# The experts' stage of a hybrid encoder layer: down products moved behind the next pair's gate and up, and a second tile for one expert alone

## The chip, the cores and the metric

The kernel runs on one core of one Trainium2 chip. The metric is the time of one execution on the device in microseconds (us); 1420.89 us is the median of three runs before the change. Engines are called by their short names: PE (TensorE, matrix products), PEld (its weight loads), DVE (VectorE), ACT (ScalarE), POOL (GpSimd), SP (SyncE, which here issues transfers).

## The reference

The layer mixes tokens (neighbourhood attention beside a gated delta rule) and then sends each of 1024 tokens to two of 64 SwiGLU experts. Only the second half bears on the change:

```
def hierarchical_moe(h, wg_r, bg_r, we_r, be_r, w_gate, w_up, w_down):
    ...
    top_val, top_idx = lax.top_k(in_group, TOP_K_IN_GROUP)      # 2 of 8 experts of the token's group
    gates = gp * jax.nn.softmax(top_val, axis=-1)
    ...
    def expert_block(args):
        tok, e = args
        xb = h_pad[tok]                                          # rows of 1024
        hid = jax.nn.silu(xb @ w_gate[e]) * (xb @ w_up[e])       # 256 wide
        return hid @ w_down[e]
    ...
    y = jnp.zeros((n + 1, d_), h.dtype).at[buf_tok].add(out)[:n]
```

All weights are float32: gate and up of an expert are 2 MiB together, down is 1 MiB, so 64 experts are 192 MiB.

## The kernel before

Up to about 840 us the kernel does token mixing and routing. What follows is the experts' stage, a loop of 32 steps (`NS`). Step i takes a **pair** of experts, e and e + 32, which belong to different groups; the first tile of a pair is 128 rows, 64 (`CAP`) for each expert. For a step the kernel

- gathers the rows of the tokens by an indirect transfer that POOL issues (`gather`, L1020), three steps ahead (`LA = 3`) into four buffers `xgb`;
- transposes them on PE into `xT` (`turn`, L1028), with DVE copying out of PSUM (L1029);
- multiplies by gate and up (`pp`, L1042): 8 slices of the inner dimension for each expert, the two experts of a slice one after the other on the two column halves of PE;
- forms silu(gate) * up (`sg`, ACT L1047 and DVE L1048), transposes it (`ph`, L1051; `hT`, ACT L1053);
- multiplies by down (`po`, L1060), scales by the gate weight (`yg`, DVE L1062), and adds the rows into the output by an indirect transfer with accumulation (L1063, POOL).

`experts` writes all of this. Its argument `between` is the transposes of the next step's rows, which are written behind the gate and up products; in the last step it is None, and then the products are ordered by expert (L1040) instead of alternating:

```
        if between is None:
            order.sort(key=lambda kd: kd[1])
```

If one expert of the pair has more than 64 tokens (`more[i] > CAP`, L1112), a **second tile** follows at the end of the step: `experts` once more with 128 rows for both experts, out of the same buffer `xgb` (L1086, L1113). By the counts that the reference's own inputs give, this happens in steps 0, 8, 15, 19, 23 and 24; in step 15 both experts have more than 64 tokens, in the five others one has. Every engine evaluates the branch in every step.

**Loads.** SP issues the weights. Gate and up go into seven buffers (`wg`), down into six (`wd`), `room = (7, 6)`. Experts 0 to 4 are loaded before the loop; POOL issues three loads at its start, because in step 0 `eng` is pool. Then each step issues four, in an order set by `loads`: wg, wd, wd, wg. A load waits until the products that read its buffer are done, those of a second tile too, and until the load eight places ahead of it has landed.

Of the kernel before, what the change touches and what calls it, by code (L numbers as in the profile page):

```python
# [19 lines left out]
P = 128  # L20
# [16 lines left out]
def tile_layer(ctx, tc, a, out):  # L37
# [930 lines left out]
    for f, t in [(None, 0)] + tail:  # L968
        ins = f(t) if f else last
        if f is None or f is ao_mm and t in (4, 6, 7):  # L970
            e = pace.pop(0)
            wt.setdefault(e % 32, []).append(load_w(mwA, e, after=ins))
        if f is ao_mm and t == NT - 1:

            opj.close()
            mwB = ctx.enter_context(tc.tile_pool(name="mwB", bufs=1, side="right", reuse_waits="tile"))
            m1 = ctx.enter_context(tc.tile_pool(name="m1", bufs=1, side="right", reuse_waits="tile"))
            wt.setdefault(steps[2][1], [[], []])[0] += load_w(mwB, steps[2][1], after=ins)
            tS = [m1.tile([P, 32, 4], I32, name=f"tS{i}") for i in range(2)]
# [4 lines left out]
            for x in xgb:  # L984
                pool.memset(x, 0.0)

    for tl in range(2):
        for d in range(2):
            src = tab[tl * CAP:(tl + 1) * CAP, d * 32:(d + 1) * 32]
            dst = tS[tl][d * 64:(d + 1) * 64]  # L990
            dve.tensor_scalar(dst[:, :, 0], src[:, :, 0], OOB, None, op0=OP.add)
            dve.tensor_copy(dst[:, :, 2:4].bitcast(F32), src[:, :, 1:3])
# [4 lines left out]
    ci = cst.tile([1, 128], I32, name="ci")  # L997
# [4 lines left out]
    dve.tensor_tensor(ci[:, 0:32], cnt[:, 0:32], cnt[:, 32:64], op=OP.max)  # L1002
    pool.iota(lim, pattern=[[CAP, 14]], base=2 * CAP, channel_multiplier=0, allow_small_or_imprecise_dtypes=True)
# [29 lines left out]
    def experts(ws, meta, xT, gp, between=None):  # L1033
# [7 lines left out]
        for k, d in order:  # L1041
            pe.matmul(pp[d * CAP:(d + 1) * CAP], xT[:, k, d * CAP:(d + 1) * CAP],  # L1042
                      ws[d][0][:, :, k * 256:(k + 1) * 256], start=(k == 0), stop=(k == NK - 1))
# [4 lines left out]
        dve.scalar_tensor_tensor(sg[:n], pp[:n, 1], mf[:n, 3:4], sg[:n], op0=OP.mult, op1=OP.mult)  # L1048
        ph = psX.tile([P, 2, P], F32, name="ph", bufs=1)
# [3 lines left out]
        act.activation(hT[:, :, :n], ph[:, :, :n], AF.Copy)  # L1053
        yg = m2.tile([P, D], F32, name="yg", bufs=3)
# [8 lines left out]
        ins = pool.indirect_dma_start(out=out, out_offset=bass.IndirectOffsetOnAxis(ap=meta[:n, 0:1], axis=0), in_=yg[:n],  # L1063
                                      in_offset=None, bounds_check=S - 1, oob_is_err=False, compute_op=OP.add)
        if gp is None:
            return
        for g, ii in rows.items():
            if g != gp:
                for i in ii:
                    tc.declare_no_dep(ins.ins, i.ins, reason="rows of the tokens of other groups")  # L1070
        rows[gp].append(ins)
# [22 lines left out]
    second(0)  # L1094
    for i in range(NS):
        gp, e = steps[i]
        args = (pool, ins, mybir.DependencyClass.NoSync) if i == 0 else ()
        for n, part in loads[i and first + 4 * (i - 1):first + 4 * i]:
# [5 lines left out]

        def ahead():
            if i + 1 < NS:
                xTs[i + 1] = turn(xgb[(i + 1) % (LA + 1)], P)

        experts(wt[e], tS[0][:, e], xTs[i], gp, ahead if i + 1 < NS else None)
        if i + 1 < NS:  # L1110
            second(i + 1)
        with tc.If(more[i] > CAP):  # L1112
            experts(wt[e], tS[1][:, e], turn(xgb[i % (LA + 1)], P), gp, list)  # L1113
    rest = nc.values_load(ci[:, 32:33], min_val=0, max_val=S)
    with tc.If(rest > 0):
        with tc.For_i(0, 64) as e:
            left = nc.values_load(ci[:, bass.ds(e + 64, 1)], min_val=0, max_val=14)
            with tc.For_i(0, left) as i:
# [4 lines left out]
                experts([w], meta, turn(xgb[0], CAP), None)  # L1123
# [67 lines left out]
```

## Time and profile before

| | |
|---|---|
| three runs | 1419.18, 1420.89, 1422.25 us |
| the profiled execution | 1420.96 us; its span, first to last instruction, 1419.2 us |
| PE busy over the span | 1232.4 us (87%) |
| DVE, ACT, POOL busy | 658.2 us (46%), 393.8 us (28%), 378.1 us (27%) |
| loads of expert weights that SP issues | wg x62 (2048 KB each, median 34.5 us to landing), wd x63 (1024 KB, 33.5 us) |
| second tiles | 38 calls of L1047 and of L1063 for 32 steps: 6 |

Times in rows are counted from the span's start. "Landing" is the end of a transfer; a busy share is a mean over a stretch, and says nothing of what was waited for. The profiled execution stands 1.76 us above its span, and 0.07 us above the median of the runs.

### The profile page before, as it was taken

The numbers are of one execution on the slowest core, as the hardware profiler recorded it, in microseconds if no ns is written. First come the engines' busy times: TensorE is split into PE (matmuls) and PEld (weight loads), VectorE is DVE, ScalarE is ACT, GpSimd is POOL, SyncE is SP. The second block draws the span as 40 slices with busy tenths as digits, with TensorE's granted clock in tenths as the row PEclk, the third lists the DMA queues.
The fourth block names the chain that finished last, engine by engine and source line by source line (L and its number), as shares of the span: only waits on it lengthen the run. The fifth ranks groups of instructions, "written<-read, shape, count | busy, mean of one in ns | idle before, by whom it ended". The sixth has DMA issues, their size and how long they took to land. (4 is left out here: it accounts for less than half of the span.)

```text
span 1419.2 us, 20349 instructions
## 1 busy us (share of the span) xinstructions
PE 1232.4 (87%) x7313; PEld 829.9 (58%) x7314; DVE 658.2 (46%) x1629; ACT 393.8 (28%) x798; POOL 378.1 (27%) x428
## 2 busy tenths in 40 slices
PE   6987999969989996688989968998888989989985
PEld 6866889969978895466768843333322333323331
DVE  5566853753667652667867862222211221212211
ACT  6445422322344431766445310000000000000000
POOL 1147313021655544112210351211211121111200
PEclk9998999989999997799989979999999999999998
DMA  4251246346565469997793988999999999998981
GB/s 157 61 124 43 71 134 171 98 138 146 166 173 149 116 176 219 300 254 210 176 258 105 343 299 311 384 409 399 414 408 407 375 404 372 388 356 325 385 330 21
DMA packets 110134, 346.80 MB, mean 244 GB/s; under 512 B 43312, under 2 KB 49456, under 8 KB 93376
## 3 DMA queue, kind: packets, MB, share of 16 engines
q1 hardware_dynamic: 74480, 260.68, 51.0%
q0 software_dynamic: 27264, 68.80, 18.6%
q10 hardware_dynamic: 8272, 15.78, 3.1%
q8 instruction: 71, 1.16, 0.3%
q14 instruction: 47, 0.39, 0.1%
HBM read 305.26 MB, written 62.98 MB: 259 GB/s over the span
## 5 line engine op out<-in xcount | busy, mean ns | idle before, releaser
L1042 PE MATMUL pp<-wg,xT 128*64 128x512 f32 x1216 | 295.9, 615 | 35.8 <-DMA wg<-in_w_gu 21.0
L1042 PEld LDWEIGHTS pp<-wg,xT 128*64 128x64 f32 x1216 | 98.2, 141 | 227.9 <-issue 185.5
L1063 POOL DMA_INDIRECT out<-yg,tS x38 | 60.4, 1589 | 412.5 <-DVEq L1112 267.2
L1048 DVE SCALAR_TENSOR_TENSOR sg<-pp,tS,sg 128x256 f32<-128x256 f32 x38 | 18.4, 483 | 312.3 <-ACT sg L1047 312.3
L1060 PE MATMUL po<-wd,hT 128*64 128x512 f32 x608 | 140.5, 605 | 20.4 <-ACTq L1112 14.2
L1047 ACT ACTIVATE sg<-pp,tS 128x256 f32<-128x256 f32 x38 | 18.0, 474 | 483.4 <-PE pp L1042 483.4
L84 PE MATMUL pA<-w_hi,h_hi 128*128 128x256 f32 x512 | 150.4, 294 | 0.0
L85 PE MATMUL pA<-w_lo,h_hi 128*128 128x256 f32 x512 | 149.4, 292 | 0.0
L86 PE MATMUL pA<-w_hi,h_lo 128*128 128x256 f32 x512 | 149.4, 292 | 0.0
L1062 DVE TENSOR_SCALAR yg<-po,tS 128x512 f32<-128x512 f32 x76 | 57.0, 750 | 119.9 <-PE po L1060 119.9
L84 PEld LDWEIGHTS pA<-w_hi,h_hi 128*128 128x128 f32 x512 | 99.9, 195 | 0.7 <-issue 0.2
L86 PEld LDWEIGHTS pA<-w_hi,h_lo 128*128 128x128 f32 x512 | 99.7, 195 | 0.3
L85 PEld LDWEIGHTS pA<-w_lo,h_hi 128*128 128x128 f32 x512 | 99.8, 195 | 0.2
L1060 PEld LDWEIGHTS po<-wd,hT 128*64 128x64 f32 x608 | 40.6, 138 | 94.0 <-issue 66.4
L85 PE MATMUL pA<-h_lo,w_hi 128*128 128x512 f32 x192 | 77.4, 403 | 0.0
L84 PE MATMUL pA<-h_hi,w_hi 128*128 128x512 f32 x192 | 77.4, 403 | 0.0
L86 PE MATMUL pA<-h_hi,w_lo 128*128 128x512 f32 x192 | 76.8, 400 | 0.0
L76 DVE TENSOR_TENSOR w_lo<-w_raw,w_hi 128x512 fp32r<-128x512 f32 x56 | 38.7, 702 | 72.6 <-ACT w_hi L75 70.6
L250 DVE SCALAR_TENSOR_TENSOR acc<-raw,convw,acc 128x1024 f32<-128x1024 f32 x48 | 63.2, 1319 | 13.1 <-ACT acc L248 12.7
L84 PE MATMUL pA<-wo_hi,t_hi 128*128 128x512 f32 x128 | 55.1, 430 | 6.9 <-ACT t_hi L750 5.9
L1028 PEld LDWEIGHTS pt<-ident,xg 128*128 128x128 f32 x304 | 37.5, 195 | 37.6 <-issue 30.0
L665 PE MATMUL pv<-pT,vw 128*128 128x256 f32 x192 | 53.5, 415 | 2.5 <-ACT pT L656 1.6
(322 smaller groups left out, 2297.5 us busy)
## 6 DMA issues: line engine op xcount, KB each, us to landing
wg<-in_w_gu SPq DMA_DIRECT2D x62, 2048.0 KB, 34.5
wd<-in_w_down SPq DMA_DIRECT2D x63, 1024.0 KB, 33.5
bt<-in_bias SPq DMA_DIRECT2D x24, 384.0 KB, 5.5
w_raw<-in_w_nat SPq DMA_DIRECT2D x32, 256.0 KB, 3.4
w_raw<-in_w_dn SPq DMA_DIRECT2D x24, 256.0 KB, 3.4
k<-kk_d POOLq DMA_DIRECT2D x16, 384.0 KB, 10.2
SA_d<-cm POOLq DMA_DIRECT2D x8, 512.0 KB, 2.9
kk_d<-ev POOLq DMA_DIRECT2D x8, 512.0 KB, 4.4
```

Source lines behind the costliest of these rows:

```text
L76: dve.tensor_sub(lo[:, k:k + 2], raw, hi[:, k:k + 2].bitcast(F32))
L84: pe.matmul(dst, sh, mh, start=(i == 0), stop=False)
L85: pe.matmul(dst, sh, ml, start=False, stop=False)
L86: pe.matmul(dst, sl, mh, start=False, stop=(i == n - 1))
L250: dve.scalar_tensor_tensor(acc, raw[:, t:t + S], convw[:, m, t:t + 1], acc, op0=OP.mult, op1=OP.add)
L665: pe.matmul(pv, vw[:, w, half + g, pr * P:(pr + 1) * P], pT[:, g], start=(g == 0), stop=(g == 2))
L1028: pe.transpose(pt[:, k, :n], xg[:n, g * 4 + k:D:NK], ident[:n, :n])
L1042: pe.matmul(pp[d * CAP:(d + 1) * CAP], xT[:, k, d * CAP:(d + 1) * CAP], ws[d][0][:, :, k * 256:(k + 1) * 256], start=(k == 0), stop=(k == ...
L1048: dve.scalar_tensor_tensor(sg[:n], pp[:n, 1], mf[:n, 3:4], sg[:n], op0=OP.mult, op1=OP.mult)
L1060: pe.matmul(po[d * CAP:(d + 1) * CAP], hT[:, k, d * CAP:(d + 1) * CAP], w[1][:, k * D + c * 512:k * D + (c + 1) * 512], start=(k == 0), st ...
L1062: dve.tensor_scalar(yg[:n, cs], po[:n], mf[:n, 2:3], None, op0=OP.mult)
L1063: ins = pool.indirect_dma_start(out=out, out_offset=bass.IndirectOffsetOnAxis(ap=meta[:n, 0:1], axis=0), in_=yg[:n], in_offset=None, bound ...
```

## The change

A step is cut into `gate_up`, `turn_h`, `down` and `add_rows`. The down products of step i are now written behind gate and up of step i + 1 (`finish`). The second tile stands right behind gate and up of its own step, gathers into a buffer of its own (`xg2`, named xs) in two halves, and calls `second_tile` only for the expert that overflows: gate goes to one column half of PE and up to the other, 256 columns each, and the two halves of down's columns likewise. The list of loads is replaced by `upto`: the loads of a step are two wg and the two wd that came free one step later. `LA` is 2, `xT` has two buffers.

```
-            LA = 3
+            LA = 2
...
+            xg2 = m1.tile([P, D], F32, name="xs")
...
+    dve.tensor_copy(ci[:, 128:192], cnt)
...
-        xT = m2.tile([P, NK, P], F32, name="xT", bufs=3)
+        xT = m2.tile([P, NK, P], F32, name="xT")
...
-        order = [(k, d) for k in range(NK) for d in range(len(ws))]
-        if between is None:
-            order.sort(key=lambda kd: kd[1])
...
-        if between:
-            between()
+        for k in range(NK):
+            for d in range(len(ws)):
+                pe.matmul(pp[d * CAP:(d + 1) * CAP], xT[:, k, d * CAP:(d + 1) * CAP],
+                          ws[d][0][:, :, k * 256:(k + 1) * 256], start=(k == 0), stop=(k == NK - 1))
...
+    def second_tile(w, d, meta, xT, gp):
...
+        pp = psX.tile([P, 2, 256], F32, name="pp")
+        for k in range(NK):
+            for i in range(2):
+                pe.matmul(pp[hs[i], i], xT[:, k, mine], w[0][:, i, k * 256:(k + 1) * 256], start=(k == 0), stop=(k == NK - 1))
...
+        yg = m2.tile([P, D], F32, name="yg", bufs=3)
+        po = psX.tile([P, 512], F32, name="po")
+        for k in range(2):
+            for c in range(2):
+                pe.matmul(po[hs[c]], hT[:, k], w[1][:, k * D + c * 512:k * D + (c + 1) * 512],
+                          start=(k == 0), stop=(k == 1))
...
+        add_rows(yg[me], meta[me, 0:1], gp, (d,))
...
-    loads = [(2 * j + d, part) for j in range(2, NS) for part in range(2) for d in range(2)]
-    loads = [l for l in loads if l[0] != 4]
-    first = next(i for i, (n, part) in enumerate(loads) if n == room[part])
+    loaded = [[0, 1, 2, 3, 4], [0, 1, 2, 3, 4]]
+
+    def upto(i):
+
+        todo = []
+        for part in (1, 0):
+            n1 = min(2 * NS, room[part] + 2 * max(0, i - part))
+            todo += [(n, part) for n in range(2 * NS) if n < n1 and n not in loaded[part]]
+            loaded[part] += [n for n, p in todo if p == part]
+        return sorted(todo, key=lambda l: (l[0] + 3 * l[1], l[1]))
...
-            gather(xgb[i % (LA + 1)], tS[1][:, e], P)
+            for d in range(2):
+                gather(xg2[d * CAP:(d + 1) * CAP], tS[1][:, e + 32 * d], CAP)
...
+    def finish(i):
+        gp, e = steps[i]
+        down(wt[e], tS[0][:, e], hTs.pop(i), gp)
...
+        sg = gate_up(wt[e], tS[0][:, e], xTs.pop(i))
+        with tc.If(more[i] > CAP):
+            xT = turn(xg2, P)
+            for d in range(2):
+                c = nc.values_load(ci[:, 128 + e + 32 * d:129 + e + 32 * d], min_val=0, max_val=S)
+                with tc.If(c > CAP):
+                    second_tile(wt[e][d], d, tS[1][:, e + 32 * d], xT, gp)
         if i + 1 < NS:
             second(i + 1)
-        with tc.If(more[i] > CAP):
-            experts(wt[e], tS[1][:, e], turn(xgb[i % (LA + 1)], P), gp, list)
+        if i > 0:
+            finish(i - 1)
+        hTs[i] = turn_h(sg, P)
+        if i + 1 < NS:
+            xTs[i + 1] = turn(xgb[(i + 1) % (LA + 1)], P)
+    finish(NS - 1)
```

PE, one step in the steady part, before (L1042 gate and up, L1028 the next rows' transposes, L1084 and L1085 the branch on POOL's gather, L1051 and L1060 the step's own down, L1112 the branch of the second tile):

```order
L1042 MATMUL pp<-wg,xT 64x512 x16
L1028 MATMUL pt<-ident,xg_8039 128x128 x8
L1084 TENSOR_LOAD ci
L1085 COMPARE_AND_BRANCH
L1085 UNCONDITIONAL_BRANCH x2
L1051 MATMUL ph<-ident,sg 128x128 x2
L1060 MATMUL po<-wd,hT 64x512 x8
L1112 COMPARE_AND_BRANCH
L1028 MATMUL pt<-ident,xg_8038 128x128 x8
L1042 MATMUL pp<-wg,xT 64x512 x16
```

and now (L1076 the down products of the step before, L1051 the transposes for this step's own, L1029 the next rows, L1041 gate and up of the next step, L1155 its second tile, L1159 the expert):

```order
L1076 MATMUL po<-wd,hT 64x512 x8
L1051 MATMUL ph<-ident,sg 128x128 x2
L1029 MATMUL pt<-ident,xg_8038 128x128 x8
L1041 MATMUL pp<-wg,xT 64x512 x16
L1155 COMPARE_AND_BRANCH
L1029 MATMUL pt<-ident,xs 128x128 x8
L1158 TENSOR_LOAD ci
L1159 COMPARE_AND_BRANCH
L1089 MATMUL pp<-wg,xT 64x256 x16
L1095 MATMUL ph<-ident,sg_13485 128x64 x2
L1102 MATMUL po<-wd,hT_13491 64x512 x4
```

The second tile's branch, behind which the buffers of `wg` come free in a step without one, stood at the end of a step's down products and stands now right behind its gate and up.

SP, the last loads, before:

```order
L958 DMA wg<-in_w_gu 128x4096
L958 DMA wd<-in_w_down 128x2048 x2
L1085 COMPARE_AND_BRANCH
L1085 UNCONDITIONAL_BRANCH x2
L958 DMA wg<-in_w_gu 128x4096
L1112 COMPARE_AND_BRANCH
L1112 UNCONDITIONAL_BRANCH x2
L958 DMA wg<-in_w_gu 128x4096
L958 DMA wd<-in_w_down 128x2048 x2
```

and now:

```order
L958 DMA wd<-in_w_down 128x2048
L958 DMA wg<-in_w_gu 128x4096
L958 DMA wd<-in_w_down 128x2048
L958 DMA wg<-in_w_gu 128x4096
...
L1128 COMPARE_AND_BRANCH
L1128 UNCONDITIONAL_BRANCH x2
L958 DMA wd<-in_w_down 128x2048 x2
L1127 ISA x2
L958 DMA wd<-in_w_down 128x2048 x2
```

The last wg was third from the end with two wd behind it; now four wd stand behind it, and the four before alternate.

## Rows read from the trace of the kernel before

**Rows 1.** Busy time by stretches: PE, PEld, DVE, ACT, POOL, then clock, DMA, GB/s.
```profile
1050.00:1100.00 50.00, 39.82 (x166) 13.88 (x164) 9.54 (x15) 2.58 (x6) 8.78 (x7) 0.93 1.01 410
1375.00:1394.00 19.00, 18.16 (x64) 6.10 (x61) 3.18 (x5) 0.86 (x2) 1.56 (x1) 0.90 0.23 83
```

**Rows 2.** Waits of SP, 850 to 1420 us: total us, times, longest.
```profile
SPq L958 <- DMA wg<-in_w_gu: 203.6, 43, 6.7
SPq L958 <- PEq L1112: 88.7, 13, 11.4
```

**Rows 3.** Loads that SP issues, in order of time: start, us, count.
```profile
870.90 0.34 SPq L958 DMA_DIRECT2D wg<-in_w_gu  x1
...
890.91 12.01 SPq L958 DMA_DIRECT2D wg<-in_w_gu  x2
...
1021.84 5.98 SPq L958 DMA_DIRECT2D wg<-in_w_gu  x2
...
1240.08 6.24 SPq L958 DMA_DIRECT2D wg<-in_w_gu  x2
```

**Rows 4.** Time to landing by tile wg or wd: all wg, then single loads by window.
```profile
DMA to landing us min/median/max: 7.7/34.4/39.0
...
L958 POOL DMA_DIRECT2D wg<-in_w_gu x1: 558/558/558, 850.5 to 850.5; - x1
DMA to landing us min/median/max: 14.4/14.4/14.4
L958 SPq DMA_DIRECT2D wg<-in_w_gu x1: 328/328/328, 902.6 to 902.6; - x1
DMA to landing us min/median/max: 14.6/14.6/14.6
L958 SPq DMA_DIRECT2D wg<-in_w_gu x1: 328/328/328, 1354.8 to 1354.8; - x1
DMA to landing us min/median/max: 34.0/34.0/34.0
L958 SPq DMA_DIRECT2D wd<-in_w_down x1: 328/328/328, 1360.9 to 1360.9; - x1
DMA to landing us min/median/max: 32.9/32.9/32.9
```

**Rows 5.** PE in order of time: a second tile (step 8), then plain steps.
```profile
984.32 1.16 PE L1028 MATMUL pt<-ident,xg 128*128 128x128 f32 x8
985.84 7.09 PE L1042 MATMUL pp<-wg,xT 128*64 128x512 f32 x32 [0.36 <-DVE xT L1029]
994.05 0.51 PE L1051 MATMUL ph<-ident,sg 128*128 128x128 f32 x2 [1.12 <-DVE sg L1048]
995.09 3.65 PE L1060 MATMUL po<-wd,hT 128*64 128x512 f32 x16 [0.53 <-ACT hT L1053]
998.57 7.04 PE L1042 MATMUL pp<-wg,xT 128*64 128x512 f32 x32
...
1314.93 7.09 PE L1042 MATMUL pp<-wg,xT 128*64 128x512 f32 x32 [0.31 <-PEq L1112]
```

**Rows 6.** PE in order of time: step 0 and its second tile.
```profile
855.16 1.16 PE L1028 MATMUL pt<-ident,xg 128*128 128x128 f32 x8
863.79 7.09 PE L1042 MATMUL pp<-wg,xT 128*64 128x512 f32 x32 [0.42 <-DVE xT L1029]
```

**Rows 7.** PE in order of time: the end of the kernel.
```profile
1354.50 7.31 PE L1042 MATMUL pp<-wg,xT 128*64 128x512 f32 x32 [0.31 <-PEq L1112]
1372.87 9.97 PE L1042 MATMUL pp<-wg,xT 128*64 128x512 f32 x30 [3.78 <-SPq L1115]
1388.92 12.26 PE L1042 MATMUL pp<-wg,xT 128*64 128x512 f32 x32 [0.31 <-PEq L1112]
1403.30 3.65 PE L1060 MATMUL po<-wd,hT 128*64 128x512 f32 x16 [0.53 <-ACTq L1112]
```

**Rows 8.** The adding transfers, 900 to 1380 us, by tile: time to landing.
```profile
DMA to landing us min/median/max: 10.6/12.1/13.9
```

More of the change, by code (lines that the diff above doesn't have):

```diff
@@ L978, in tile_layer @@
             wt.setdefault(steps[2][1], [[], []])[0] += load_w(mwB, steps[2][1], after=ins)
-            tS = [m1.tile([P, 32, 4], I32, name=f"tS{i}") for i in range(2)]
+            tS = [m1.tile([P, 32, 4], I32, name="tS"), m1.tile([CAP, 64, 4], I32, name="t2")]
             ln2p = m1.tile([P, NK], F32, name="ln2p")
             act.dma_start(ln2p, a["ln2"][:, 1])
-            LA = 3
+            LA = 2
             xgb = [m1.tile([P, D], F32, name=f"xg{i}") for i in range(LA + 1)]
-            for x in xgb:
+            xg2 = m1.tile([P, D], F32, name="xs")
+            for x in (*xgb, xg2):
                 pool.memset(x, 0.0)
[L987 to L992, printed above, removed]
+    for tl, d in ((0, 0), (0, 1), (1, 0)):
+        src = tab[tl * CAP:(tl + 1) * CAP, d * 32:(d + 1 + tl) * 32]
+        dst = tS[tl][d * CAP:(d + 1) * CAP]
+        dve.tensor_scalar(dst[:, :, 0], src[:, :, 0], OOB, None, op0=OP.add)
+        dve.tensor_copy(dst[:, :, 2:4].bitcast(F32), src[:, :, 1:3])
     cnt = rc.tile([1, 64], F32, name="cnt")
@@ L996, in tile_layer @@
     over = o2.tile([P, D], F32, name="x2", bufs=5)[0:1, :64 * 14].rearrange("p (e i) -> p e i", i=14)
-    ci = cst.tile([1, 128], I32, name="ci")
+    ci = cst.tile([1, 192], I32, name="ci")
     pn = psQ.tile([P, P], F32, name="pv", bufs=1)
@@ L1031, in turn, with gate_up @@
         return xT
-    def experts(ws, meta, xT, gp, between=None):
+    def gate_up(ws, meta, xT):
         n = CAP * len(ws)
@@ L1053, in experts, with add_rows, down @@
         act.activation(hT[:, :, :n], ph[:, :, :n], AF.Copy)
+        return hT
+    def add_rows(yg, idx, gp, ds):
+        ins = pool.indirect_dma_start(out=out, out_offset=bass.IndirectOffsetOnAxis(ap=idx, axis=0), in_=yg,
+                                      in_offset=None, bounds_check=S - 1, oob_is_err=False, compute_op=OP.add)
+        if gp is None:
+            return
+        for g, ii in rows.items():
+            for i, di in ii:
+                if g != gp or not set(ds) & set(di):
+                    tc.declare_no_dep(ins.ins, i.ins, reason="rows of the tokens of other groups")
+        rows[gp].append((ins, ds))
+    def down(ws, meta, hT, gp):
+        n = CAP * len(ws)
+        mf = meta.bitcast(F32)
         yg = m2.tile([P, D], F32, name="yg", bufs=3)
@@ L1062, in experts @@
             dve.tensor_scalar(yg[:n, cs], po[:n], mf[:n, 2:3], None, op0=OP.mult)
[L1063 to L1070, printed above, removed]
@@ L1071, in experts @@
-        rows[gp].append(ins)
+        add_rows(yg[:n], meta[:n, 0:1], gp, (0, 1))
+    def second_tile(w, d, meta, xT, gp):
+        hs = [slice(0, CAP), slice(CAP, 2 * CAP)]
+        me, mine = hs[0], hs[d]
+        mf = meta.bitcast(F32)
+        pp = psX.tile([P, 2, 256], F32, name="pp")
+        for k in range(NK):
+            for i in range(2):
+                pe.matmul(pp[hs[i], i], xT[:, k, mine], w[0][:, i, k * 256:(k + 1) * 256], start=(k == 0), stop=(k == NK - 1))
+        sg = m2.tile([CAP, 256], F32, name="sg2", bufs=1)
+        act.activation(sg[:], pp[me, 0], AF.Silu, scale=mf[me, 3:4])
+        dve.scalar_tensor_tensor(sg[:], pp[hs[1], 1], mf[me, 3:4], sg[:], op0=OP.mult, op1=OP.mult)
+        ph = psX.tile([P, 2, P], F32, name="ph", bufs=1)
+        for k in range(2):
+            pe.transpose(ph[:, k, :CAP], sg[:, k:256:2], ident[me, me])
+        hT = m2.tile([P, 2, CAP], F32, name="hT2", bufs=1)
+        act.activation(hT, ph[:, :, :CAP], AF.Copy)
+        yg = m2.tile([P, D], F32, name="yg", bufs=3)
+        po = psX.tile([P, 512], F32, name="po")
+        for k in range(2):
+            for c in range(2):
+                pe.matmul(po[hs[c]], hT[:, k], w[1][:, k * D + c * 512:k * D + (c + 1) * 512],
+                          start=(k == 0), stop=(k == 1))
+        for c in range(2):
+            dve.tensor_scalar(yg[me, c * 512:(c + 1) * 512], po[hs[c]], mf[me, 2:3], None, op0=OP.mult)
+        add_rows(yg[me], meta[me, 0:1], gp, (d,))
@@ L1097, in tile_layer @@
         args = (pool, ins, mybir.DependencyClass.NoSync) if i == 0 else ()
-        for n, part in loads[i and first + 4 * (i - 1):first + 4 * i]:
+        for n, part in upto(i):
             f = steps[n // 2][1]
@@ L1122, in tile_layer @@
                 gather(xgb[0], meta, CAP)
-                experts([w], meta, turn(xgb[0], CAP), None)
+                down([w], meta, turn_h(gate_up([w], meta, turn(xgb[0], CAP)), CAP), None)
 def layout(inputs):
```

10 lines of the change are left out of this document (3 added, 7 removed).

## The prediction

> **What bounds the kernel now.** I read the stretches first [rows 1]. Around 1050 to 1100 us the DMA share is 1.01 at 410 GB/s while PE is busy for 39.82 of 50 us: the transfers are the scarce thing there. SP's waits say the same [rows 2]: 203.6 us of them are for an earlier load to land and 88.7 us for PE to pass the second tile's branch (L1112), so most loads are issued the moment another lands. Then the pace of the two sides. From the pair of wg loads at 1021.84 to the one at 1240.08 [rows 3] there are twelve steps, 18.19 us each, although two second tiles (steps 15 and 19) fell between. PE by itself needs (1354.50 - 1314.93) / 3 = 13.19 us for a step [rows 5, 7]. A second tile adds 998.57 - 984.32 = 14.25 us [rows 5], 85 us over all six, and the gaps it makes are absorbed as long as loads are queued: the median wg lands 34.4 us after its issue [rows 4], almost two steps.
>
> So the kernel's end is made of two pieces: when the last load lands, and what PE does after that. The last wd is issued at 1360.9 and lands 32.9 us later, at **1393.8** [rows 4]; the span ends at 1419.2, **25.4 us** later. In between, the DMA share is already low (0.23 in 1375 to 1394 [rows 1]), but landing is what PE waits for, and a load lands when its slowest part does: at 1372.87 PE goes on when a wg has landed that has two more wg and four wd behind it [rows 7].
>
> The rate of the load stream: the wg issued at 890.91 + 12.01 less its own third of a microsecond, that is 902.6, lands at 902.6 + 14.6 = 917.2 [rows 3, 4]; it belongs to expert 11 of the order, counted from 0. Behind it come wg 12 to 63 and wd 10 to 63, 52 * 2 + 54 = 158 MiB, in 1393.8 - 917.2 = 476.6 us: **3.02 us per MiB**, 18.1 per step, the same as SP's pitch. From 917 us on the stream never paused, so work taken off PE there moves nothing.
>
> **The change, part by part.**
>
> *Down moved behind the next gate and up.* Per step PE still has 32 + 16 matmul records, two and eight transposes. What goes are the 0.53 us before the down products (hT) and what comes is the wait for xT behind the transposes, 0.36 us [rows 5]; the branch's 0.31 us stays and its two inner branches stand inside a block that is skipped. About 13.1 us per step: nothing, hidden by the 18.1 us of loads. If that cover were gone the gain would be 0.1 us per step.
>
> *The second tile for one expert.* 256 columns per matmul do not occur in the trace. Below, half of 7.09 us is 3.55; above, the same 32 records at the same price, 7.09. The eight transposes with 128 columns take 1.16 us, 0.145 each [rows 5], which for 32 records is 4.6 us; I take that. With the rest of the tile (1.16 + 0.36 transposes, 1.12 + 0.51 + 0.53 around sg and hT, half of 3.65 for down, two branches at 0.31) it is 10.7 us against 14.25, and 19.3 for step 15, where it runs twice. PE saves 5 * 3.5 - 5 = 12 us, all but step 0 under the loads.
>
> *The start.* Here the loads do wait for PE. The last load that POOL issues, at 850.5, lands at 864.9 [rows 4]. The next one needs the buffer that step 0's second tile still reads, and that tile's gate and up run from 863.79 for 7.09 us [rows 6]; so it is issued at 870.90 [rows 3] and, by the shortest landing of all wg, 7.7 us [rows 4], is there at 878.6. From 864.9 to 917.2, 52.3 us, wg 7 to 11 and wd 6 to 9 come in, 14 MiB, which at 3.02 is 42.3: **10.0 us are lost**. Now the second tile starts where the transposes of the next rows stood, at 855.2 [rows 6], its rows being in a buffer of their own: 855.2 + 1.5 + 4.6 = 861.3 (860.2 to 863.8 by the bounds) frees the first buffer, 865.8 the second. wg 7 then lands about 869, wg 8 and the wd that POOL issues late, behind this branch, by 878; step 1's gate and up end about 875 and free the next. I find some 1.5 us still lost, so **8.5 us come back** (10 at most; 4 if the tile is at its dear bound and the branches' register loads cost a microsecond each). Later wd loads cost nothing: wd is needed a step later too, and is asked for two steps ahead as before. The last landing moves from 1393.8 to 1385.3.
>
> *The end.* Before, the last step's products were ordered by expert and took 12.26 us instead of 7.09, without overlap of the column halves; and gate and up of the step before, at the low clock after its wait, 9.97 us [rows 7]. The wg for the last step landed at 1354.8 + 34.0 = 1388.8, 5.0 us before the end of the stream [rows 4], so a MiB takes 2.5 us there. Now four wd stand behind the last wg: it lands 10 us before the last wd, the one before it 17.5 to 18. Counted from the last landing: gate and up of step 31 from -9.7 to -2.6, branch to -2.3, down of step 30 to +1.4, transposes +1.9, hT +2.4, down of step 31 to **+6.0**. Before, down ended at 1403.30 + 3.65 = 1406.95 and the span 12.25 us later (eviction, POOL, the adding transfer and the drain); that stays. The tail is 18.3 us; if the last gate and up take 9.97 because PE waited before them, 21.2. I take **19.6** against 25.4.
>
> *Costs elsewhere.* POOL has six indirect transfers in its step instead of four, two of them skipped with the second tile and two with its gather; its step is 18 us and a transfer there 1.6, so this is hidden. LA = 2 leaves the gather about two PE steps less a few microseconds, over 20 us. The yg buffers are a new wait: three are taken per step out of three, so the eviction of a step needs the adding transfer of the step before to have landed, 10.6 to 13.9 us after its issue [rows 8]. With two evictions (1.5) and POOL's start (0.3) that is a loop of 13.9, at most 15.7: above PE's 13.1, below 18.1. Nothing while loads bound; what is late is PE by 0.7 us a step in the first few steps, where loads are queued.
>
> **Sum** against the profiled execution (1420.96, 1.76 above its span; the median of the runs is 0.07 lower): span 1385.3 + 19.6 = 1404.9, time **1406.7 us**, 14.3 less: 8.5 from the start, 5.8 from the end. Its own range is 1403.9 - 1.0 to 1412.8 (10 and 18.3; 4 and 21.2 with a microsecond of scatter).
>
> **Rivals.** (A) *The start gives nothing*: POOL's late wd, or the nested branch, holds the early loads as long as now. For it: SP's 88.7 us on the branch show how a branch holds loads. Against: it is passed 10 us sooner. Time 1393.8 + 19.6 + 1.76 = 1415.2.
>
> [...]
>
> (C) *Slower*: the loop through yg becomes the bound. Its price from the point where it decides: an adding transfer that lands later than 16.3 us after its issue makes the loop longer than 18.1 us. For it: the transfers now share the queue with a stream that never pauses early, and POOL issues more. Against: the longest of 33 is 13.9 [rows 8], in the same saturated stretch. At 17.2 us, a loop of 19 us, 30 steps cost 0.9 each: 27 us against 14 gained, 1434.
>
> (D) *No change*: the loads take the time that they take, and a later first release eats the shorter tail: 1420.
>
> **How the numbers follow.** The sum's own case 0.55, A 0.14, B 0.08, C 0.10, D 0.08, and 0.05 for a gain larger than the sum's range (a stream without pauses that runs at 18.0 us a step, 1400). Faster by over 0.2% (under 1418.1; about what three runs can tell from no change, since they spread by 0.2%) is the sum, A, B and the larger gain, 0.82; within it 0.08; slower 0.10. The range goes to both neighbours, 1401 to 1418: it holds the sum's case, A, B and a part of D.
>
> **What would show it.** Right: the first SP load of the loop about 861 instead of 870.90, the pitch of wg pairs still 18.2, the last wd landing about 1385, four wd behind the last wg, gate and up of the last step near 7 us and down ending 6 us behind the last landing. Wrong: a pitch above 18.5, DVE's evictions waiting for out<-yg, PE waiting for xg or xs, or a gap in the landings between 865 and 900.

## The result, and the profile after

The changed kernel takes **1407.16 us** (median of four runs, 1401.6 to 1409.91) against 1421.16 for the kernel before on the same chip: a ratio of **0.9898, 95% interval [0.9864, 0.9932]**. Run again on another chip, it gave 1406.51 against 1419.18, 0.9909 [0.9894, 0.9925]; the experiments are compared with this second ratio, each by its own ratio to the kernel before on its own chip. The profiled execution took 1408.78 us, its span 1407.0. The forecast was 1406.7 us.

Five groups of rows of the profile after answer to those of before. First the costliest groups on the page (line, engine, operation, tiles, shape, count; busy us and mean ns of one; idle us just before them and what ended most of it):

```profile
L1041 PE MATMUL pp<-wg,xT 128*64 128x512 f32 x1024 | 233.1, 604 | 19.7 <-DVE xT L1030 19.4
L1076 PE MATMUL po<-wd,hT 128*64 128x512 f32 x512 | 126.8, 622 | 45.1 <-DVEq L1155 28.3
L1078 DVE TENSOR_SCALAR yg<-po,tS 128x512 f32<-128x512 f32 x64 | 47.0, 749 | 126.2 <-DMA out<-yg,tS 66.8
```

Of the 19.7 us that PE sits idle ahead of gate and up (L1041), 19.4 are for xT and none to speak of for wg; the down products (L1076) wait 28.3 us for DVE to pass the second tile's branch (L1155), and DVE's evictions (L1078) wait for the adding transfers. Next the loads that SP issues (start, us, count), which answer to [rows 3, 4]:

```profile
861.72 14.72 SPq L958 DMA_DIRECT2D wg<-in_w_gu  x3
...
1348.06 14.62 SPq L958 DMA_DIRECT2D wd<-in_w_down  x4
```

The first is issued at 861.72 instead of 870.90, and four wd stand behind the last wg. Then PE in step 0 (start, us; in brackets the idle time before it and its releaser):

```profile
848.41 7.89 PE L1041 MATMUL pp<-wg,xT 128*64 128x512 f32 x32
858.00 3.67 PE L1089 MATMUL pp<-wg,xT 128*64 128x256 f32 x32 [0.60 <-DVE xT L1030]
863.58 1.94 PE L1102 MATMUL po<-wd,hT 128*64 128x512 f32 x8 [0.37 <-ACT hT L1097]
```

The second tile for one expert has its gate and up done in 3.67 us, half of the 7.09 before [rows 6]. The busy time by stretches (PE, PEld, DVE, ACT, POOL, clock, DMA share, GB/s) answers to [rows 1]; the first fence is of before, three stretches that were not shown, the second of after:

```profile
860.00:900.00 40.00, 36.61 (x176) 14.16 (x174) 9.59 (x15) 2.58 (x6) 6.97 (x5) 1.00 0.82 298
1100.00:1150.00 50.00, 46.07 (x212) 17.62 (x210) 11.21 (x18) 3.44 (x8) 7.06 (x6) 0.97 0.99 378
1250.00:1300.00 50.00, 44.90 (x214) 17.08 (x212) 11.21 (x18) 3.43 (x8) 6.84 (x5) 1.00 0.86 321
```

```profile
860.00:900.00 40.00, 32.54 (x158) 14.80 (x156) 9.63 (x15) 2.85 (x7) 9.19 (x8) 0.97 1.00 386
1100.00:1150.00 50.00, 38.02 (x184) 15.50 (x182) 10.33 (x16) 3.21 (x8) 8.20 (x6) 0.90 0.93 355
1250.00:1300.00 50.00, 36.83 (x176) 14.74 (x178) 11.31 (x17) 2.46 (x6) 10.13 (x8) 0.87 0.89 338
1375.00:1386.00 11.00, 9.23 (x46) 3.42 (x42) 2.80 (x5) 0.86 (x2) 1.56 (x1) 1.00 0.19 59
1387.00:1391.00 4.00, 3.54 (x18) 1.25 (x14) 1.50 (x2) 0.36 (x1) 0.00 (x0) 1.00 0.00 0
```

Between 860 and 900 us the DMA share rose from 0.82 to 1.00: 0.18 * 40 = 7.2 us of transfers come earlier. Between 1250 and 1300 the stream is not full in either kernel, and between 1100 and 1150 it is not in the changed one. Nothing moves between 1387 and 1391: the last load has landed by 1387. Last PE at a plain step late in the loop and at the end, against [rows 5, 7]:

```profile
1336.12 7.09 PE L1041 MATMUL pp<-wg,xT 128*64 128x512 f32 x32 [0.33 <-DVE xT L1030]
1349.74 7.09 PE L1041 MATMUL pp<-wg,xT 128*64 128x512 f32 x32 [0.34 <-DVE xT L1030]
1378.16 7.09 PE L1041 MATMUL pp<-wg,xT 128*64 128x512 f32 x32 [1.02 <-DVE xT L1030]
1386.45 3.65 PE L1076 MATMUL po<-wd,hT 128*64 128x512 f32 x16 [1.20 <-DVEq L1155]
1391.08 3.65 PE L1076 MATMUL po<-wd,hT 128*64 128x512 f32 x16 [0.54 <-ACT hT L1053]
```

Here lies the surprise. No product at the end waits for a wg: the last step's gate and up wait for xT, and a plain step takes 13.6 us (1336.12 to 1349.74). So PE runs from step 25 to the end without a long wait for a load, though not always at that pace: the six steps from 1291.28 to 1378.16 take 14.5 us each on average. In the longest PE waits 2.32 us for xT, because DVE's evictions, which stand ahead of xT, waited 5.40 us for an adding transfer:

```profile
1304.81 1.41 DVE L1078 TENSOR_SCALAR yg<-po,tS 128x512 f32<-128x512 f32 x2 [5.40 <-DMA out<-yg,tS]
1306.87 8.78 PE L1041 MATMUL pp<-wg,xT 128*64 128x512 f32 x32 [2.32 <-DVE xT L1030]
```

The place where PE last waits for a load for long is step 23, which has a second tile. The rows of PE from there to step 25, and below them those of step 15, the other step with such a wait:

```profile
1233.26 8.12 PE L1041 MATMUL pp<-wg,xT 128*64 128x512 f32 x32 [0.34 <-DVE xT L1030]
1254.94 3.68 PE L1102 MATMUL po<-wd,hT 128*64 128x512 f32 x8 [6.66 <-DMA wd<-in_w_down]
1260.27 5.03 PE L1076 MATMUL po<-wd,hT 128*64 128x512 f32 x16 [1.65 <-DVEq L1159]
1291.28 7.09 PE L1041 MATMUL pp<-wg,xT 128*64 128x512 f32 x32 [0.34 <-DVE xT L1030]
```

```profile
1087.96 7.09 PE L1041 MATMUL pp<-wg,xT 128*64 128x512 f32 x32 [0.34 <-DVE xT L1030]
1107.15 3.68 PE L1102 MATMUL po<-wd,hT 128*64 128x512 f32 x8 [5.19 <-DMA wd<-in_w_down]
1124.57 7.09 PE L1041 MATMUL pp<-wg,xT 128*64 128x512 f32 x32 [0.34 <-DVE xT L1030]
```

The second tile needs its wd in its own step, while the first tile's down, moved, needs it one step later; the load had been put back for the latter, and PE waits 6.66 us. That the order of the loads causes this wait is read from the code and this row; no run puts that load forward again. The 8 records behind the wait take 3.68 us instead of the 1.94 of step 0, and the 16 behind those 5.03 instead of 3.65. The granted clock, the third figure from the end, is 1.00 over the 8 records of step 0, 0.50 over those behind the wait, and 0.72 over the 16: 0.50 up to 1263.00, 0.98 from there on.

```profile
863.58:865.52 1.94, 1.94 (x8) 0.48 (x8) 0.00 (x0) 0.00 (x0) 0.00 (x0) 1.00 0.86 355
1254.94:1258.62 3.68, 3.68 (x8) 0.82 (x8) 0.00 (x0) 0.00 (x0) 0.00 (x0) 0.50 1.02 430
1260.27:1265.30 5.03, 5.03 (x17) 1.62 (x17) 0.75 (x1) 0.00 (x0) 2.43 (x2) 0.72 0.69 262
```

With gate and up of steps 0, 15, 16, 23 and 25 in the kernel before, the difference of the two spans can be put together:

```profile
846.70 8.53 PE L1042 MATMUL pp<-wg,xT 128*64 128x512 f32 x32
1096.22 1.04 PE L1042 MATMUL pp<-wg,xT 128*64 128x512 f32 x2 [0.31 <-PEq L1112]
1126.83 7.04 PE L1042 MATMUL pp<-wg,xT 128*64 128x512 f32 x32
1240.63 1.04 PE L1042 MATMUL pp<-wg,xT 128*64 128x512 f32 x2 [0.36 <-PEq L1112]
1301.51 7.04 PE L1042 MATMUL pp<-wg,xT 128*64 128x512 f32 x32
```

Counted from step 0's gate and up (846.70 before, 848.41 after; the part ahead of it took 1.7 us longer in this execution), the gate and up of step 25 start at 1301.51 - 846.70 = 454.8 before and at 1291.28 - 848.41 = 442.9 after: 11.9 us earlier. From there to the span's end it is 117.7 us before and 115.7 after, 2.0 less. 11.9 + 2.0 - 1.7 = 12.2, the difference of the spans. Seven steps before the end most of the gain is made. It did not grow evenly: counted in the same way, the changed kernel is 10.0 us ahead at step 15, 4.0 at step 16 (behind the wait of 5.19 us for wd), 9.1 at step 23 and 11.9 at step 25.

### The profile page after: what moved, and what is told of

The parts are those of the page before. It is cut to its first block, busy times and chain, and to the rows that moved or that the text cites. A ratio compares the mean times of both kernels' runs of the same rounds, so it can differ in the third digit from the quotient of the medians.

```text
span 1407.0 us, 20840 instructions
## 1 busy us (share of the span) xinstructions
PE 1194.1 (85%) x7307; PEld 828.0 (59%) x7308; DVE 660.1 (47%) x1631; ACT 393.9 (28%) x800; POOL 387.4 (28%) x435
## 5 line engine op out<-in xcount | busy, mean ns | idle before, releaser
L1041 PE MATMUL pp<-wg,xT 128*64 128x512 f32 x1024 | 233.1, 604 | 19.7 <-DVE xT L1030 19.4
L1041 PEld LDWEIGHTS pp<-wg,xT 128*64 128x64 f32 x1024 | 74.4, 139 | 156.4 <-issue 128.2
L1076 PE MATMUL po<-wd,hT 128*64 128x512 f32 x512 | 126.8, 622 | 45.1 <-DVEq L1155 28.3
L1057 POOL DMA_INDIRECT out<-yg,tS x32 | 50.8, 1587 | 291.3 <-DVE yg L1078 242.8
L1045 DVE SCALAR_TENSOR_TENSOR sg<-pp,tS,sg 128x256 f32<-128x256 f32 x32 | 15.5, 484 | 233.2 <-ACTq L1155 189.0
L1076 PEld LDWEIGHTS po<-wd,hT 128*64 128x64 f32 x512 | 42.1, 142 | 129.5 <-issue 68.4
L1078 DVE TENSOR_SCALAR yg<-po,tS 128x512 f32<-128x512 f32 x64 | 47.0, 749 | 126.2 <-DMA out<-yg,tS 66.8
L250 DVE SCALAR_TENSOR_TENSOR acc<-raw,convw,acc 128x1024 f32<-128x1024 f32 x48 | 63.2, 1320 | 12.4 <-ACT acc L248 11.9
L1053 ACT ACTIVATE hT<-ph 128x256 f32<-128x256 f32 x32 | 12.3, 384 | 191.6 <-PE ph L1051 191.6
```

What stands on the lines that cost most here:

```text
L250: dve.scalar_tensor_tensor(acc, raw[:, t:t + S], convw[:, m, t:t + 1], acc, op0=OP.mult, op1=OP.add)
L1076: pe.matmul(po[d * CAP:(d + 1) * CAP], hT[:, k, d * CAP:(d + 1) * CAP], w[1][:, k * D + c * 512:k * D + (c + 1) * 512], start=(k == 0), st ...
L1078: dve.tensor_scalar(yg[:n, cs], po[:n], mf[:n, 2:3], None, op0=OP.mult)
```

## The experiments

The theories at the start: mine was the prediction's (an earlier first release in step 0 and a shorter tail; what second tiles cost later and where the down products stand is hidden under the loads); **R1**, the gain is PE time saved in all second tiles; **R2**, the gain is the move of the down products. After the second run came **T2**: PE, not the loads, sets the time from step 24 to the end.

All twelve runs, with the ratio to the kernel before and, in the last column, the distance in us to the changed kernel's 0.9909 (times 1420; the intervals of the two ratios together make that known to 3 to 4 us):

| run | median us | ratio, 95% interval | against the changed kernel |
|---|---|---|---|
| before, last step alternating | 1416.46 | 0.9983 [0.9968, 0.9998] | (-2.4 against before) |
| both experts' second tile, steps 8 to 24 | 1417.15 | 0.9989 [0.9973, 1.0005] | +11.4 |
| both experts' second tile, step 0 | 1412.13 | 0.9954 [0.9938, 0.9971] | +6.4 |
| down in its own step | 1411.41 | 0.9941 [0.9920, 0.9963] | +4.5 |
| changed kernel again | 1406.51 | 0.9909 [0.9894, 0.9925] | 0 |
| both tiles, steps 23 and 24 | 1413.14 | 0.9964 [0.9947, 0.9982] | +7.8 |
| both tiles, steps 8 and 19 | 1406.87 | 0.9919 [0.9899, 0.9938] | +1.4 |
| second tile's PSUM apart | 1408.03 | 0.9929 [0.9907, 0.9952] | +2.8 |
| its PSUM and its rows apart | 1409.98 | 0.9927 [0.9905, 0.9948] | +2.6 |
| last step by expert | 1410.96 | 0.9939 [0.9924, 0.9954] | +4.3 |
| down ahead of the branch | 1407.10 | 0.9916 [0.9900, 0.9932] | +1.0 |
| second tile whole, as before | 1419.92 | 1.0004 [0.9990, 1.0019] | +13.5 |

**The order of the last step.** In the kernel before:

```diff
-        experts(wt[e], tS[0][:, e], xTs[i], gp, ahead if i + 1 < NS else None)
+        experts(wt[e], tS[0][:, e], xTs[i], gp, ahead)
```

> The kernel before, with one difference: the last step's gate and up alternate between the two experts as in every other step, instead of being ordered by expert. My theory (a part of the gain is the shorter tail behind the last landing): gate and up of the last step take 7.1 us instead of 12.26, the last landing stays near 1394 us, so 5.2 us less, about 1416 us (1414 to 1417.5). Rival R1 (the gain is PE time saved in the six second tiles) and rival R2 (it is the place of the down products): neither is touched, so 1421 us, no change. A third way: the kernel's end hangs on the last wd alone and PE's order doesn't matter, also 1421.

Measured: -2.4 us by the ratio, -3.2 by the medians, half of the 5.2 forecast. And the same undone in the changed kernel:

```diff
-        for k in range(NK):
-            for d in range(len(ws)):
+        order = [(k, d) for k in range(NK) for d in range(len(ws))]
+        if apart:
+            order.sort(key=lambda kd: kd[1])
+        for k, d in order:
...
-        sg = gate_up(wt[e], tS[0][:, e], xTs.pop(i))
+        sg = gate_up(wt[e], tS[0][:, e], xTs.pop(i), i == NS - 1)
```

> The changed kernel, with the last step's gate and up ordered by expert again, as before the change. The prediction's tail term (12.26 instead of 7.09 us behind the last wg): +5 us, 1412. If the last wd's landing hides it (wd 63 lands when gate and up end plus 1.6 us): +3 to +4. No effect: 1407.

Measured: +4.3. PE at the end of the first run, then of the second:

```profile
1388.75 8.16 PE L1042 MATMUL pp<-wg,xT 128*64 128x512 f32 x32 [0.31 <-PEq L1112]
```

```profile
1376.40 12.29 PE L1043 MATMUL pp<-wg,xT 128*64 128x512 f32 x32 [0.34 <-DVE xT L1030]
```

In the kernel before the alternating burst takes 8.16 us, so 12.26 - 8.16 = 4.1 could be had; in the changed one it is 12.29 against 7.09. That term stands, at 2 to 4 us as measured, with an uncertainty of 2 to 3.

**Second tiles where they might be hidden, and the start.** The inner branch of the changed kernel, in steps after 0, in step 0 alone, in steps 23 and 24, and in 8 and 19:

```diff
-                with tc.If(c > CAP):
+                with tc.If(c > CAP if i == 0 else more[i] > CAP):
```

```diff
+                with tc.If(more[i] > CAP if i == 0 else c > CAP):
```

```diff
+                with tc.If(more[i] > CAP if i in (23, 24) else c > CAP):
```

```diff
+                with tc.If(more[i] > CAP if i in (8, 19) else c > CAP):
```

> The changed kernel, but in the five steps with a second tile after step 0 (8, 15, 19, 23, 24) the second tile is done for both experts, as before the change did; the tile of the expert that does not overflow is extra work whose rows are all dropped. Step 0 stays as changed, step 15 did both already. PE gets some 8 us more in each of steps 8, 19, 23 and 24, 33 us in all. My theory (after step 0 the loads bound, so what second tiles cost or save there is hidden): no change, 0 to +5 us on 1407. Rival R1 (the gain is PE's time in all second tiles): +25 to +33 us, 1432 to 1440. Rival R2 (the place of down): no change.

> The changed kernel, but in step 0 alone the second tile is done for both experts; the tile of the expert that does not overflow is extra work whose rows are all dropped. All other steps stay as changed. My theory (the start gives 7 us because step 0's buffers come free earlier): step 0's second expert's tile, the down products and all that PE does behind it come some 8 us later, and with them the second and the following loads' buffers, though the first load's buffer is free as early as now; +4 to +8 us, about 1413. Rival (the start gives nothing, the gain is all in the tail): no change, 1407. Rival R1 (gain is PE's time in all second tiles): +6 us of the 33 in all, the same as my theory, told apart from it by the run with both tiles in the later steps.

The first missed: 0 to +5 said, +11.4 measured. The second came as said, +6.4 (+4 to +8 said): the DMA share between 860 and 900 us fell from 1.00 to 0.85:

```profile
860.00:900.00 40.00, 33.62 (x172) 15.13 (x173) 9.01 (x14) 2.82 (x8) 8.30 (x7) 1.00 0.85 308
```

The first wg was issued nearly as early as in the changed kernel (859.61, 14.6 us behind step 0's gate and up, against 13.3), and still the time went: not the first release counts alone but those of the buffers behind it. To see which of the later tiles cost the 11.4 us, the changed kernel ran again beside a run of two of these steps; a run of two others followed.

> The changed kernel unaltered, beside the next three on one chip, since the run with both tiles in the later steps cost about 10 us where I had said nothing, and its comparison was with another chip's run. If that cost is real: 1407 (ratio to before 0.988 to 0.992). If it is the chip's spread: 1411 to 1413.

> The changed kernel with the second tile done for both experts in steps 23 and 24 alone (the tile of the expert that doesn't overflow is extra work whose rows are dropped): some 16 us of PE. My new theory (T2): after step 24 PE runs to the end without waiting for a wg, so what PE spends in these two steps is late at the end; the loads fall behind in turn, since their buffers come free later: +7 to +10 us on the changed kernel. The recorded prediction's view (the loads bound, later second tiles are hidden): 0 to +2. Rival R1 (every second tile counts in full): +16.

> The changed kernel with the second tile done for both experts in steps 8 and 19 alone (extra work whose rows are dropped), again some 16 us of PE, but with steps behind them in which PE waits for wd or the DMA share is 1.0. T2 (a second tile counts only if PE runs without a load's wait from there to the end): 0 to +3 on 1407, against +6.6 for the same work in steps 23 and 24. If second tiles count wherever they stand (R1): +6 or more here too. The two together cost 10 to 11 us.

Measured: the changed kernel again 0.9909, so the cost of the later tiles is real; +7.8 for steps 23 and 24, +1.4 for 8 and 19, with as much extra work in each: twice 7.4 us (below, 1287.72 to 1295.08). So the prediction's view fails in the last steps, R1 fails in the others, and T2 gave both numbers. Steps 23 to 25 with both tiles:

```profile
1252.16 3.68 PE L1102 MATMUL po<-wd,hT 128*64 128x512 f32 x8 [6.66 <-DMA wd<-in_w_down]
...
1287.72 3.62 PE L1089 MATMUL pp<-wg,xT 128*64 128x256 f32 x32
1295.08 3.81 PE L1076 MATMUL po<-wd,hT 128*64 128x512 f32 x16
1300.55 1.94 PE L1041 MATMUL pp<-wg,xT 128*64 128x512 f32 x8 [0.33 <-DVE xT L1030]
```

From the moment when wd has come to step 25's gate and up it is 1300.55 - 1252.16 = 48.4 us, against 1291.28 - 1254.94 = 36.3 in the changed kernel: 12.1 more. From there to the end it is 110.6 us, against 115.7: 5 are made good, most of them in the two steps from 1291.28 on, which were long in the changed kernel (the wait of 2.32 us for xT and a burst of 8.78 us instead of 7.09) and are shorter here. The rest stays.

**The place of down.** In the changed kernel, the products of a pair behind the next rows' transposes in their own step:

```diff
-        if i > 0:
-            finish(i - 1)
-        hTs[i] = turn_h(sg, P)
         if i + 1 < NS:
             xTs[i + 1] = turn(xgb[(i + 1) % (LA + 1)], P)
-    finish(NS - 1)
+        hTs[i] = turn_h(sg, P)
+        finish(i)
```

> The changed kernel, but the down products of a pair stand in their own step again, behind the transposes of the next rows, instead of behind the next pair's gate and up. The second tiles, the loads and their order stay as changed. My theory (the move is worth nothing, because loads hide it): within 4 us of 1407, perhaps 1 to 3 us less, since only one burst of down products then stands behind the last gate and up. Rival R2 (the gain is the move of down): all 14 us come back, 1421. In the trace: PE's pitch where it bounds, near the end, at or under 13.2 to 13.6 us by the first, above 14.2 by the second.

Measured: +4.5, just outside the 4 us allowed and with one of the widest intervals; six runs spread from 1405 to 1416. R2's 14 us are excluded, a gain of a few us by the move is not. PE still waits 27.9 us for DVE's branch there, but at the transposes instead of the down products, and a plain step takes 13.6 us there too.

**The wait at the branch.** Buffers of their own for the second tile's down products, then for its rows too:

```diff
-        po = psX.tile([P, 512], F32, name="po")
+        po = psX.tile([P, 512], F32, name="po2", bufs=1)
```

```diff
     def down(ws, meta, hT, gp):
...
-        yg = m2.tile([P, D], F32, name="yg", bufs=3)
+        yg = m2.tile([P, D], F32, name="yg")
...
     def second_tile(w, d, meta, xT, gp):
...
-        yg = m2.tile([P, D], F32, name="yg", bufs=3)
+        yg = m2.tile([CAP, D], F32, name="yg2", bufs=1)
```

> The changed kernel, with the second tile's down products in a PSUM buffer of their own, so that the first down product of a step need not wait until DVE has passed the second tile's branch (1.2 us in each step, 27 us in all). If PE bounds from step 24 to the end (T2): the wait goes, PE's pitch there falls from 13.6 to about 12.4, seven such steps are 8 us, of which the landing of the last wg (1375.8, 2.4 us before its gate and up) lets 2 to 5 through: 1402 to 1405. If the loads bound: no change, 1407. If the wait only moves on to the next product that shares a buffer with the second tile, as it did to the transposes in the run with down in its own step: no change and the same 1.2 us in another row.

> As the run before, and the second tile's output rows also in a buffer of their own, the other products having two: DVE's evictions no longer wait for the adding transfer of the step before (62 us in 17 waits), and xT comes in time (PE waits for it 0.3 to 2.3 us a step, 16 us in all). If that loop is what holds PE's pitch above 13.2: another 0.3 to 1 us a step where PE bounds, 2 to 4 us less than the run before, 1399 to 1403. If the loop is hidden, or two buffers make it tighter: no change to +3 against the run before.

Then the next rows' transposes and the down products moved ahead of the branch (from step 1 on); the second tile's PSUM buffer for its transposes and its output rows are apart there too (not shown):

```diff
+        if i > 0:
+            xTs[i + 1] = turn(xgb[(i + 1) % (LA + 1)], P) if i + 1 < NS else None
+            finish(i - 1)
         with tc.If(more[i] > CAP):
...
-        if i > 0:
-            finish(i - 1)
         hTs[i] = turn_h(sg, P)
```

> The changed kernel with the next rows' transposes and the down products of the pair before ahead of the second tile's branch (but not in step 0), the second tile's PSUM buffer for hT's transposes and its output rows apart, so that no PE work stands behind a wait of the branch. PE's pitch where it bounds: 7.09 + 1.06 + 3.65 + 0.3 + 0.5 = 12.6 instead of 13.6, seven to eight such steps from step 24 to the end: -2 to -6 us, 1401 to 1405. Against it: the branch is passed 4.8 us later in its step, the wg buffers come free that much later, and the stream's pauses (DMA share 0.89 in 1250 to 1300) grow: +2 to +6, 1409 to 1413. I hold the two about equally likely.

None was faster: +2.8, +2.6 and +1.0, none of them clear of zero. In the changed kernel PE waited 28.3 us at the down products for DVE's branch. What it waits for at a branch between 900 and 1400 us (total us, times, longest) with the PSUM apart, with the rows apart too, and with down ahead of the branch:

```profile
PE ph L1051 <- DVE yg L1078: 12.8, 11, 1.3
PE ph L1051 <- PEq L1127: 11.7, 10, 1.3
```

```profile
PE ph L1051 <- DVEq L1155: 24.3, 21, 1.2
```

```profile
PE pp L1041 <- PEq L1127: 23.1, 20, 1.3
```

The wait left the row where it stood and came back in the next product in line: in the first two at hT's transposes (1.1 us in each plain step), in the last at gate and up (1.12 us, for PE's own sequencer at the branch around the next gather, L1127). A plain step takes 13.4 us in the first two and 1329.69 - 1316.37 = 13.3 in the last, where I had said 12.6, against 13.6. With the rows apart DVE's 61.9 us of waits for the adding transfer went as well, and the time didn't fall. PE's steps are a little shorter, and then it waits near the end, with the rows apart for a wd:

```profile
1379.57 0.61 PE L1076 MATMUL po<-wd,hT 128*64 128x512 f32 x1 [1.94 <-DMA wd<-in_w_down]
```

In the last kernel it waits 2.74 us in the midst of a burst of down products (1369.46); the row names SP's sequencer, so that this was for a wd too is likely, not shown.

**The second tile as before.** In the changed kernel, one pass of 128 rows for both experts instead of the half tiles (with the index table and the gather of before):

```diff
-            for d in range(2):
-                c = nc.values_load(ci[:, 128 + e + 32 * d:129 + e + 32 * d], min_val=0, max_val=S)
-                with tc.If(c > CAP):
-                    second_tile(wt[e][d], d, tS[1][:, e + 32 * d], xT, gp)
+            meta = tS[1][:, e]
+            down(wt[e], meta, turn_h(gate_up(wt[e], meta, xT), P), gp)
```

> The changed kernel with the second tile done as before the change, one pass of 128 rows for both experts with 512 columns a matmul, but in its new place, from its own rows' buffer, and with the down products moved; this undoes the part on the second tile alone. Counted in PE: some 4.5 us more in steps 0, 8, 19, 23 and 24, 7 us less in step 15. T2 (what counts is step 0, through the loads, and steps 23 and 24, through PE's lag to the end, at the 6.6 of 16 us measured): first release about as now, the second expert's a little earlier, step 1 and what hangs on it 3 to 4 us later, and 0.41 * 9 = 3.7 us from steps 23 and 24: +4 to +7, 1411 to 1414. Rival R2 (the gain is the move of down and the new load order): no change, 1407. Rival R1 (the gain is the shorter second tiles altogether): 1419 to 1421.

Measured: 1.0004 [0.9990, 1.0019]. The whole gain is gone: R1's number, and 6 us more than T2 had said. R1's reason doesn't follow, since steps 8 and 19 had cost next to nothing. PE in step 0 and in steps 23 to 25 of this kernel:

```profile
844.08 9.19 PE L1041 MATMUL pp<-wg,xT 128*64 128x512 f32 x32
...
1255.69 1.07 PE L1076 MATMUL po<-wd,hT 128*64 128x512 f32 x2 [0.47 <-ACT hT L1053]
1261.66 8.61 PE L1076 MATMUL po<-wd,hT 128*64 128x512 f32 x30 [4.90 <-DMA wd<-in_w_down]
...
1283.45 1.94 PE L1029 MATMUL pt<-ident,xs 128*128 128x128 f32 x8 [4.42 <-DMA xs<-x_d,tS]
...
1304.91 1.51 PE L1041 MATMUL pp<-wg,xT 128*64 128x512 f32 x6 [0.33 <-DVE xT L1030]
```

Counted from step 0's gate and up (844.08 here), PE goes on behind the wait for wd at 1261.66 - 844.08 = 417.6, in the changed kernel at 1254.94 - 848.41 = 406.5: 11.1 later. Of these, 5.1 are there already at the tile's first down records (1255.69), which need the first expert's wd; this kernel issued its first load 17.7 us behind gate and up instead of 13.3, which would account for 4.4. The other 6.0 are those two records and the wait for the second expert's wd, which half a tile doesn't need. From there to step 25's gate and up it is 43.2 us against 36.3, 6.9 more, with 4.42 of it a wait for the second rows (a wait of 1.20 in the changed kernel). From there to the end 112.9 against 115.7, 2.8 less. Together 15, as the spans counted so differ (15.1). What T2 missed is the wd: it had counted PE's work in these steps and not the moment when they can begin.

## Why the prediction came out, and where it was wrong

**The time** was forecast within a microsecond. Both pieces of its sum came out near their sizes, but not by the way that the prediction gives, and that the total fits so well is in part luck.

**The start** (8.5 us given back) was right. The first load is issued at 861.72, forecast 861.3; counted from step 0's gate and up that is 13.3 us, where the forecast was 14.6 and the kernel before took 24.2. The windows show 7.2 us of transfers come earlier, and doubling the second tile there costs 6.4. The second tile's gate and up were priced at 4.6 us by the row of the transposes and took 3.67, near the lower bound of 3.55: half the columns, 256 instead of 512, took about half of the 7.09 us. The dear end of the range took a microsecond for the register load of a branch; no run shows that, PE's at the second tile's inner branch took 0.30 us (median, the longest 0.33).

**The end** (5.8 us less behind the last landing) came out near its size. The last load has landed by 1387, forecast 1385.3, and the span ends at least 20.0 us later, forecast 19.6. The order of the last step is worth 4.3 us: in the kernel before, six alternating records took 1.51 us together (from 1314.93), three ordered by expert 1.47 (from 1388.92). Down ends at 1391.08 + 3.65 = 1394.73, 12.3 us ahead of the span's end, as forecast (12.25). The granted clock was 1.00 between 1375 and 1386 and over both bursts of down, and gate and up took 7.09 us, each burst of down 3.65. In the kernel before it was 0.71 over the 9.97 us behind the wait, 0.50 up to 1377. The chance named B is that of the last bursts at a lower granted clock, for 1413 us; this did not come about.

**The step that failed** is what stands between these two: "From 917 us on the stream never paused, so work taken off PE there moves nothing." The stream did pause, with a share of 0.86 between 1250 and 1300 us in the kernel before, a stretch between the two whose shares the prediction drew on; in the changed kernel it pauses there (0.89) and between 1100 and 1150 (0.93) as well. So the 8.5 us were not carried to the end untouched: of the 10.0 us that the changed kernel is ahead at step 15, 6.0 are lost in that step alone, where PE waits for wd, and 5.1 of them are back at step 23. The forecast counted step 15's second tile as hidden, and it has neither this loss nor the later gain; that they nearly cancel is luck. From step 25 on PE was no longer held by the loads, and both ends lie close together in either kernel: before, PE ran at 13.2 us a step to 1368.05 and then waited 3.78 us [rows 7]; now the last wd is there by 1387, and PE comes to it at 1391.08.

**The second tile** (12 us saved on PE, "all but step 0 under the loads") was the mis-sized term. In steps 8 and 19 doubling it is hidden, 1.4 us for some 15 of work (twice 7.4). In steps 23 and 24 it isn't, 7.8 for as much: about half. Done whole, everywhere, it takes the gain away.

**"Later wd loads cost nothing: wd is needed a step later too"** failed in two of the steps with a second tile: PE waits 6.66 us in step 23 and 5.19 in step 15. This ate most of what the shorter tiles saved in steps 23 and 24: from step 23's gate and up to step 25's the kernel before took 60.9 us, the changed one 58.0.

**The move of down** was said to leave a step at 13.1 us, at no gain and no cost. It left 13.6: the 0.53 for hT went, as said, and 1.20 at the branch came, which I had put at 0.31. That sum took the branch's row from a place where only the branch stood; now DVE's product for sg and a register load lie on the way too (last section). Putting down back costs 4.5 +- 4 us; whether the move itself gains anything stays open.

**The yg loop** exists: DVE waits 61.9 us for the adding transfers, which the prediction had named as a sign of being wrong. For most of the loop it is hidden; behind step 25 it reaches PE, with the wait of 2.32 us for xT. Taken away, it gave no time; PE then waited for a wd near the end. Rival C's price, a loop longer than a step of loads, was not seen, and it was rightly held small. Rival A fell with the first load, rival D with the time.

The parts undone or spoiled one by one cost 6.4 (start), 7.8 (two late tiles), 4.3 (order) and 4.5 (down), 23 us in all, against a gain of 13 to 14.5. A reading that fits, argued and not tested, is that the loads and PE are within a few microseconds of each other at the end: spoiling either is felt, and improving one alone stops at the other, as the wait for a wd near the end suggests. No version tried beats the changed kernel.

## What to carry to other kernels

Where transfers and an engine are both nearly full over a stretch, ask for the last place where the engine waited for a load, and count forward from there: extra work behind that place counted for about half here (7.8 of some 15 us), work ahead of it was hidden (1.4 of 15). The exception is work that holds the first loads' buffers while nothing else is queued, as in step 0 (6.4 us). Read the DMA share in every window up to the end before calling a stream continuous. When a consumer is moved back, look for a second consumer of the same buffer that was not moved, here the second tile's use of wd (waits of 6.66 and 5.19 us). And giving one product a buffer of its own did not take a wait at a branch away: in three tries the wait came back at the next product, at 1.1 to 1.2 us a step.

## What the runs showed of the hardware

Two skipped blocks between its products cost PE 1.1 to 1.3 us in each plain step in five kernels, whichever product stood first behind them. The releaser named is DVE's sequencer in three of them (the changed kernel, down in its own step, PSUM and rows apart) and PE's own in the two others (PSUM apart, where DVE's evictions are named as often, and down ahead of the branch). In the kernel before, where a branch stood alone, it was 0.31 us. In the run with the second tile whole it was 1.6 to 2.0 us in five steps near the end and 0.4 to 0.5 in the last two, which stays open. Two rows of the changed kernel tell what it is made of:

```profile
1385.81 0.48 DVE L1045 SCALAR_TENSOR_TENSOR sg<-pp,tS,sg 128x256 f32<-128x256 f32 x1 [7.10 <-ACTq L1155]
L1127 PEldq TENSOR_LOAD <-ci x32: 297/303/488, 846.0 to 1372.2; - x32
```

DVE passes the branch behind its product for sg, which ends 1.04 us behind the last gate and up (1385.81 + 0.48 against 1378.16 + 7.09): 0.16 of the 1.20 us are left for the branch itself. PE's own sequencer has a register load of 0.30 us on its way, and branches of 0.33 (L1155) and 0.21 (L1128), medians. So there seem to be two ways of similar length, which would fit that freeing one product from DVE left the wait at 1.1; it was not tested apart. DVE's compare and branch there takes 0.06 us (L1155, median).

Behind the wait of 6.66 us the burst's 8 records took 3.68 us at a granted clock of 0.50, where those of step 0 took 1.94 at 1.00; behind the wait of 5.19 us in step 15 it was 3.68 us at 0.50 too. The next 16 records of step 23 took 5.03 us at 0.72, against 3.65 at 1.00 at the end. By the difference the lower clock cost about 1.7 and 1.4 us, an estimate from these rows.
